# Layer 0's modulation vectors on four column groups of TensorE in half blocks, instead of VectorE ticks

## The chip, the cores and the metric

The kernel runs on one core of a Trainium2 chip. The core has TensorE (PE, matrix products; its weight loads are listed as PEld), VectorE (DVE), ScalarE (ACT), GpSimd (POOL) and a DMA queue that SyncE (SP) issues in order. The metric is the device time of one execution in microseconds (us), lower is better; a median over runs is given, and one execution is profiled.

## The reference, cut to what matters

Two layers of a trunk over 512 latent and 256 context tokens of width 1024. Each layer begins with a modulation: six vectors of 1024 for the latent tokens (from `c`) and six for the context tokens (from `c_ctx`).

```
m   = silu(c)     @ w_mod[l] + b_mod[l]      # (1024) @ (1024, 6144), split into six vectors
m_c = silu(c_ctx) @ w_mod[l] + b_mod[l]
h   = rms_norm(x, g_mix) * (1 + scale1) + shift1
x   = x + gate1 * mixer(h)                   # layer 0: SSD heads and RG-LRU blocks
h   = rms_norm(x, g_ffn) * (1 + scale2) + shift2
x   = x + gate2 * conv_ffn(h)
```

So `w_mod` of each layer, 24 MB, is read once and multiplied with two vectors only. Vectors 0 and 1 are needed before the mixer's projections, vector 2 at its output, 3 and 4 for the norm before the FFN, 5 at the FFN's output.

## The kernel before

`w_mod[l]` is cut into 24 column blocks `j` of 256 columns, four to each of the six vectors. There are three ways to compute a block.

- **On TensorE, `mod_now`** (L291): a 1 MB panel `st` is loaded, eight matmuls with the two columns `sc[:, k]` as weights and 256 columns of `w_mod` as moving data give `pmod` (2x256); VectorE copies it out (L276), two small transposes `pmodt` (L258) turn it, VectorE adds the bias (L261). Layer 0's blocks 0 to 7 go this way before the first projection, and block 21 in the output phase.
- **On VectorE, `mod_tick`** (L325): a tick loads 128 rows x 256 columns (`mst`, 128 KB, two buffers) and does two SCALAR_TENSOR_TENSORs, one for each vector, into `macc` (L83 is the helper's line). After eight ticks four matmuls with a column of ones (L352) sum over the partitions and VectorE adds the bias (L354). Layer 0's other 15 blocks (120 ticks) and all of layer 1's go this way.
- `mod_split` and `mod_vec` exist and are not used.

Work after the first norm runs in phases: the convolved projections `xbc` (from about 62 us), with the S5 tables of layer 1 and the first SSD steps woven in; the RG-LRU phase `lru_phase` (L1337), whose step for a block n projects `u` and the gate, computes four gate products (L1274, L1275), a recurrence on VectorE, ScalarE and GpSimd (L1300 to L1310) and every second n a `z` panel; the output phase `rout_phase` with the backward SSD; `project`; then FFN 0 from about 770 us. Each loop calls `mtick` with a number of ticks out of the table `MT`: one per block or step in `xbc` and `lru`, 4.5 per output block, 6 per block in `project`, 5 per step in FFN 0. The scheduler that emits the program then places each engine's instructions in an order of its own; an engine works strictly in that order, and SP too. PSUM tiles called `ps` have three buffers for `pmod`, `pmodt` and the SSD's products together.

A weight panel is loaded into `st` (two buffers), split by ScalarE (`whi`) and VectorE (`wlo`, L193), and each 128 rows of output take matmuls of 512 columns (`px`) and 256 columns (`pc`), three for each of eight k.

Of the kernel before, what the change touches and what calls it, by code (L numbers as in the profile page):

```python
# [64 lines left out]
def build(tc, I, out, dbg=None):  # L65
# [186 lines left out]
    def mod_finish(l, j, row, n, m):  # L252

        i, k0 = (j * 2) // 8, (j * 2) % 8
        r = n * m
        pt = pss("pmodt")
        for h_ in range(2):
            PE.transpose(pt[:, r * h_:r * h_ + r], row[:r, h_ * 128:(h_ + 1) * 128], ident[:r, :r])  # L258
        if m == 1:
            for h_ in range(2):  # L260
                V.tensor_scalar(MOD[l][i][:, k0 + h_, 0:n], pt[:, r * h_:r * h_ + r], P("bm", l * 48 + j * 2 + h_), None, op0=ALU.add)  # L261
        else:
            tmp = sm.tile([128, 8], F32, tag="mtmp", name="mtmp", bufs=2)
            V.tensor_copy(tmp, pt[:, :8])
            for h_ in range(2):
                stt(MOD[l][i][:, k0 + h_, :], tmp[:, 4 * h_:4 * h_ + 2], P("bm", l * 48 + j * 2 + h_), tmp[:, 4 * h_ + 2:4 * h_ + 4], ALU.add, ALU.add)
# [7 lines left out]
    def mod_row(ps, r):  # L274
        row = macc()[:, 0]
        V.tensor_copy(row[:r], ps[:r, :256])  # L276
        return row

    def mod_split(l, j, eng=None):

        w = wpanel(I["w_mod"][l], 0, 8, j * 256, 256, byk=True, eng=eng)
# [5 lines left out]
        row = mod_row(ps, 4)
        PEND.append({"l": l, "j": j, "stages": [lambda: mod_finish(l, j, row, 2, 2)]})

    def mod_now(l, j, st=None):  # L290

        if st is None:
            if (l, j) not in MODP:
                return
            st = wload(I["w_mod"][l], 0, 8, j * 256, 256)
        ps = pss("pmod")
        for k in range(8):
# [9 lines left out]

    PE_ = [j for j in range(8, 20) if (0, j) in MODP]

    def mod_pe(at):  # L310

        if at in PNS and PE_:
            k = PNS[at]
            (mod_now(0, PE_.pop(0)) if k == 1 else mod_split(0, PE_.pop(0), G if k == 2 else V))
# [41 lines left out]

    def mod_vec(l, j, st):

        acc = macc()
        for k in range(8):  # L360
            for e in range(2):
                stt(acc[:, e], st[:, k, :], sc[:, k, e:e + 1], zero.broadcast_to([128, 256]) if k == 0 else acc[:, e], ALU.mult, ALU.add)
        mod_pend(l, j, 2, acc, 1)
# [172 lines left out]
    def mod0(i):
        if START[i] == 1:
            mod_now(0, J0[i], ST0.pop(i))
        elif START[i] == 3:
            mod_vec(0, J0[i], ST0.pop(i))  # L540
        else:
            mod_split(0, J0[i], G if START[i] == 2 else V)

# [20 lines left out]
    for c in range(6):  # L564
        xturn(c)
        if c == LP0:

# [1 line left out]
            act(sc[:, :, 0], PS("c", 0, 8), AF.Silu)
            act(sc[:, :, 1], PS("cc", 0, 8), AF.Silu)  # L570
            V.tensor_copy(sc4[:, :, 0:2], sc)
            V.tensor_sub(sc4[:, :, 2:4], sc, sc4[:, :, 0:2].bitcast(F32))
# [1538 lines left out]
```

## Time and profile before

| | us |
|---|---|
| median of 3 runs (2154.59 to 2159.02) | 2155.79 |
| the profiled execution | 2153.56 |
| its span in the trace | 2151.8 |
| PE busy (94%) | 2024.4 |
| PEld busy (79%) | 1698.0 |
| DVE busy (73%) | 1573.4 |
| ACT busy (41%) | 878.2 |
| POOL busy (13%) | 278.9 |

"Busy" is the time in which at least one instruction of the engine is under way; matmuls are pipelined, so a busy PE need not be at its peak. PEclk is the clock that TensorE was granted, as a share of full speed. In the profile's page the 40 slices of PE read 8 or 9 but for a 4 in the third; those of DVE read 9 in slices 3, 5, 6 and 7. The 1.8 us between span and execution time lie outside the trace.

### The profile page before, as it was taken

How to read it: one execution, taken by the hardware profiler on the slowest of the kernel's cores; microseconds unless marked ns; L12 is line 12 of the kernel's file. 1: busy time of each engine (PE TensorE's matmuls, PEld its weight loads, DVE VectorE, ACT ScalarE, POOL GpSimd, SP SyncE). 2: the span in 40 equal slices, each digit the busy share in tenths (PEclk: the TensorE clock that was granted, in tenths of full speed). 3: DMA queues.
4: the chain of work that ended last, by engine and by line, in shares of the span. 5: the costliest groups of instructions: out<-in, count | busy, mean ns of one | idle time of the engine just before them, and what ended most of it. 6: DMA issues, size and time to landing. Idle time of an engine off the chain costs nothing.

```text
span 2151.8 us, 32734 instructions
## 1 busy us (share of the span) xinstructions
PE 2024.4 (94%) x12738; PEld 1698.0 (79%) x12738; DVE 1573.4 (73%) x2956; ACT 878.2 (41%) x1280; POOL 278.9 (13%) x240
## 2 busy tenths in 40 slices
PE   8949889888898999999999999999999899999998
PEld 4838778877677888888888888887887688888887
DVE  5897999867778888867775655665876768667484
ACT  4624577686624452212221223324444434223234
POOL 2061432334531000000000000020001100000000
PEclk9979989999899999999999999999999999999999
DMA  9425634425666414333234213455422122222221
GB/s 329 124 82 169 190 109 150 139 89 157 229 215 220 129 50 137 98 121 120 94 106 130 74 59 99 127 150 151 135 77 67 40 79 98 82 95 98 98 84 54
DMA packets 283018, 261.09 MB, mean 121 GB/s; under 512 B 23405, under 2 KB 263060, under 8 KB 282864
## 3 DMA queue, kind: packets, MB, share of 16 engines
q1 hardware_dynamic: 257504, 243.35, 35.7%
q10 hardware_dynamic: 24464, 13.75, 2.2%
q8 instruction: 100, 1.64, 0.3%
q0 software_dynamic: 896, 1.90, 0.2%
q14 instruction: 54, 0.44, 0.1%
HBM read 224.17 MB, written 34.78 MB: 120 GB/s over the span
## 4 chain that ended last, share of the span: by engine, by line
PE 62%; DVE 5%; DMA 3%; issue 2%; POOL 1%; ACT 1%; SPq 0%; POOLq 0%; DVEq 0%; ACTq 0%
PE px L215 33%; PE pc L215 10%; PE pu L215 6%; PE pseg L215 4%; DMA mst<-in_w_mod_dram 2%; DVE macc L83 1%; PE pmodt L352 1%; PE pv L222 1%; PE pv L223 1%; PE pv L224 1%; PE pob L215 1%; DMA x_d<-xo 0%; DMA Nt<-n_d 0%; DVE kx L1900 0%; PE plv L1856 0%
## 5 line engine op out<-in xcount | busy, mean ns | idle before, releaser
L80 ACT ACTIVATE whi<-st 128x1024 fp32r<-128x1024 f32 (+1 forms) x197 | 203.4, 1037 | 562.8 <-PE pc L215 367.0
L215 PE MATMUL px<-HH,whi 128*128 128x512 f32 (+2 forms) x1016 | 408.9, 404 | 19.1 <-DVE xbct L83 11.7
L215 PE MATMUL px<-HL,whi 128*128 128x512 f32 (+2 forms) x1016 | 404.6, 399 | 0.8 <-DVE HL L83 0.8
L215 PE MATMUL px<-HH,wlo 128*128 128x512 f32 (+2 forms) x1016 | 404.9, 399 | 0.0
L193 DVE TENSOR_TENSOR wlo<-st,whi 128x1024 fp32r<-128x1024 f32 (+1 forms) x197 | 238.5, 1213 | 77.6 <-ACT whi L80 75.5
L83 DVE SCALAR_TENSOR_TENSOR macc<-mst,sc,macc 128x256 f32<-128x256 f32 x434 | 218.4, 534 | 68.9 <-DMA mst<-in_w_mod_dram 68.0
L83 DVE SCALAR_TENSOR_TENSOR fa<-px,par,fa 128x441 f32<-128x441 f32 (+2 forms) x352 | 241.8, 691 | 8.2 <-ACT fa L80 2.2
L215 PEld LDWEIGHTS px<-HH,whi 128*128 128x128 f32 (+1 forms) x1016 | 192.7, 190 | 63.5 <-DVE xbct L83 12.1
L215 PEld LDWEIGHTS px<-HL,whi 128*128 128x128 f32 (+1 forms) x1016 | 192.6, 190 | 44.8 <-DVE HL L83 1.9
L215 PEld LDWEIGHTS px<-HH,wlo 128*128 128x128 f32 (+1 forms) x1016 | 192.4, 189 | 44.1
L215 PE MATMUL pc<-HH,whi 128*128 128x256 f32 x728 | 207.9, 287 | 14.1 <-DVE xbct L83 7.7
L215 PE MATMUL pc<-HL,whi 128*128 128x256 f32 x728 | 206.8, 285 | 0.0
L215 PE MATMUL pc<-HH,wlo 128*128 128x256 f32 x728 | 206.5, 284 | 0.0
L215 PEld LDWEIGHTS pc<-HH,whi 128*128 128x128 f32 x728 | 137.9, 190 | 18.5 <-issue 11.0
L80 ACT ACT_TABLE_LOAD x108 | 138.6, 1283 | 25.9 <-issue 6.2
L215 PEld LDWEIGHTS pc<-HL,whi 128*128 128x128 f32 x728 | 138.0, 190 | 1.2
L215 PEld LDWEIGHTS pc<-HH,wlo 128*128 128x128 f32 x728 | 137.7, 189 | 0.5
L215 PE MATMUL px<-fhi,wlo 128*128 128x512 f32 x304 | 120.4, 396 | 0.0
L215 PE MATMUL px<-fhi,whi 128*128 128x512 f32 x304 | 120.3, 396 | 0.0
L215 PE MATMUL px<-flo,whi 128*128 128x512 f32 x304 | 119.9, 394 | 0.0
L1813 POOL TENSOR_TENSOR kc<-kc,e 128x255 f32<-128x255 f32 x6 | 7.1, 1182 | 858.0 <-ACT kc L80 679.6
L215 PE MATMUL pu<-HH,wlo 128*128 128x512 f32 (+1 forms) x192 | 74.3, 387 | 0.0
(618 smaller groups left out, 4295.4 us busy)
## 6 DMA issues: line engine op xcount, KB each, us to landing
mst<-in_w_mod_dram SPq DMA_DIRECT2D x312, 128.0 KB, 2.1
st<-in_ffn_w_gate_dram SPq DMA_DIRECT2D x22, 1024.0 KB, 4.9
st<-in_ffn_w_up_dram SPq DMA_DIRECT2D x22, 1024.0 KB, 5.0
st<-in_ev_w_in_dram SPq DMA_DIRECT2D x18, 1024.0 KB, 6.3
st<-in_ffn_w_down_dram SPq DMA_DIRECT2D x16, 1024.0 KB, 5.0
bc<-cum_d SPq DMA_DIRECT2D x24, 512.0 KB, 6.1
sth<-in_od_w_in_dram SPq DMA_DIRECT2D x24, 512.0 KB, 4.0
st<-in_w_mod_dram SPq DMA_DIRECT2D x9, 1024.0 KB, 10.2
```

The lines of the kernel that those rows point to most:

```text
L80: return S.activation(o, i, f, bias=bias, scale=scale, **kw)
L83: return (eng or V).scalar_tensor_tensor(o, a, s, b, op0=op0, op1=op1)
L193: (eng or V).tensor_sub(lo, src, hi.bitcast(F32))
L215: PE.matmul(o, ww[:, k, :M], hh[k][part][:, sl], start=(first and q == 0 and a == 0), stop=(stop and q == last and a == 2))
L222: PE.matmul(o, hh[k][0][:, sl], whi[:, k % 4, :], start=(k == 0), stop=False)
L223: PE.matmul(o, hh[k][0][:, sl], wlo[:, k % 4, :], start=False, stop=False)
L224: PE.matmul(o, hh[k][1][:, sl], whi[:, k % 4, :], start=False, stop=(k == 7))
L352: PE.matmul(pt[:, 2 * h_ + e:2 * h_ + e + 1], acc[:, e, h_ * 128:(h_ + 1) * 128], ones[:, 0:1], start=True, stop=True)
L1813: G.tensor_mul(kc[:, 0, 0:255], kc[:, 0, 0:255], e0[:, 0:255])
```

## The change

Layer 0 leaves the ticks. Every block of layer 0 is now computed by `mod_half`, in two halves of 128 columns. The weights are 32 columns wide (`sc32`, of which two are not zero), and the eight matmuls of a half go to four column groups of TensorE (`tile_position=(0, 32q)`), two accumulating in each; the output is a 128x128 tile with four partial sums. ScalarE copies it to `mrow`, TensorE transposes it (128x128), VectorE sums the four parts (TENSOR_REDUCE) and adds the bias. Blocks 0 to 7 take their data from the same 1 MB panels as before; blocks 8 to 23 take 32 halves of 512 KB from a new buffer `mcol`, of which there is one. Two of three steps of `lru_phase` issue a half, then each output block; `xbc` issues none. Layer 1 keeps its ticks, and its pool `modp` is opened after `project` instead of at the start; in `xbc`, `lru`, `rout` and `project` there are no ticks any more, and the last four blocks of layer 1 that `out_first` named (and skipped) are dropped.

```diff
-MT = (1, 1, 4.5, 5, 1, 6, 1)
+MT = (5, 1)
-MODP = [(0, 21)]
+    HALVES = [(j, h_) for j in (8, 9, 10, 11, 16, 17, 18, 19, 12, 13, 14, 15, 20, 21, 22, 23) for h_ in range(2)]
...
+    def mod_half(l, j, h_, st):
+        if st is None:
+            st = mrp.tile([128, 8, 128], F32, tag="mcol", name="mcol", bufs=1)
+            c0 = j * 256 + h_ * 128
+            SP.dma_start(st, I["w_mod"][l, :, c0:c0 + 128].rearrange("(k p) c -> p k c", p=128))
         ps = pss("pmod")
         for k in range(8):
-            PE.matmul(ps[:2, :256], sc[:, k, :], st[:, k, :], start=(k == 0), stop=(k == 7))
-        row = mod_row(ps, 2)
+            q = k % 4 * 32
+            PE.matmul(ps[q:q + 32, :128], sc32[:, k, :], st[:, k, :], start=(k < 4), stop=(k >= 4), tile_position=(0, q))
+        row = mrp.tile([128, 128], F32, tag="mrow", name="mrow", bufs=2)
+        act(row, ps[:, :128], AF.Copy)
+        def finish():
+            pt = pss("pmodt")
+            PE.transpose(pt[:, :128], row, ident)
+            tmp = sm.tile([128, 2], F32, tag="mtmp", name="mtmp", bufs=2)
+            V.tensor_reduce(tmp, pt[:, :128].rearrange("p (q r) -> p r q", q=4)[:, 0:2, :], axis=mybir.AxisListType.X, op=ALU.add)
+            V.tensor_scalar(MOD[l][i][:, k0 + h_, :], tmp, P("bm", l * 48 + j * 2 + h_), None, op0=ALU.add)
...
-    MODSEQ = [(l, j) for l in range(2) for j in range(8 - 8 * l, 24) if (l, j) not in MODP]
+    MODSEQ = [(1, j) for j in range(24)]
...
+    def mod_at(go):
+        for q in list(PEND):
+            mod_advance(q)
+        if go and HALVES:
+            j, h_ = HALVES.pop(0)
+            mod_half(0, j, h_, None)
...
-                mtick(MT[0] if XI[0] >= SSD0 - 4 else MT[4])
+                mod_at(False)
...
-            mtick(MT[1])
+            mod_at(at % 3 < 2)
...
-        mod_now(0, 21)
...
-                mtick(MT[2])
+                mod_at(True)
```

On TensorE, at the start of the program: `pmod` is a panel's product, `pmodt` its transpose, `px` and `pc` the first projection. Before, then now:

```order
L428 MATMUL pnc<-diag,ones 128x256
L298 MATMUL pmod<-st,sc 2x256 x8
L258 MATMUL pmodt<-ident,macc 128x2 x2
L215 MATMUL px<-HH,whi 128x512
L215 MATMUL pc<-HH,whi 128x256
L215 MATMUL px<-HL,whi 128x512
```

```order
L408 MATMUL pnc<-diag,ones 128x256
L214 MATMUL px<-HH,whi 128x512 x2
L275 MATMUL pmod<-st,sc_114 32x128 x8
L284 MATMUL pmodt<-ident,mrow 128x128
L275 MATMUL pmod<-st,sc_114 32x128 x8
L284 MATMUL pmodt<-ident,mrow 128x128
L214 MATMUL px<-HL,whi 128x512
```

A panel is two groups of eight matmuls with a wide transpose each, and the projection begins one panel earlier.

On SP, where the RG-LRU phase begins: `gw` are the gate weights of a block, `st` a 1 MB weight panel, `yp_d` and `bc` belong to the SSD. Before, then now:

```order
L1126 DMA yp_d<-y 128x512
L322 DMA mst<-in_w_mod_dram 128x256
L182 DMA st<-in_ev_w_in_dram 128x8x256
L322 DMA mst<-in_w_mod_dram 128x256 x5
L1266 DMA gw<-in_lru_w_a_dram 128x2x128
L1267 DMA gw<-in_lru_w_i_dram 128x2x128
```

```order
L1066 DMA bc<-cum_d 128x8x128
L271 DMA mcol<-in_w_mod_dram 128x8x128
L1236 DMA gw<-in_lru_w_a_dram 128x2x128
L1237 DMA gw<-in_lru_w_i_dram 128x2x128
L181 DMA st<-in_ev_w_in_dram 128x8x256
L271 DMA mcol<-in_w_mod_dram 128x8x128 x2
L181 DMA st<-in_ev_w_in_dram 128x8x256
```

Small loads that waited for VectorE have gone from between the panels; larger ones that wait for TensorE stand there.

On DVE, in the recurrence of the third RG-LRU block: `gate` and `a` are its tiles. Before, then now:

```order
L1105 TENSOR_TENSOR bc<-bc,dtv 128x1024 x2
L83 SCALAR_TENSOR_TENSOR macc<-mst,sc,macc 128x256 x7
L83 SCALAR_TENSOR_TENSOR gate_3580<-a_3633,gate_3580 128x768
L83 SCALAR_TENSOR_TENSOR macc<-mst,sc,macc 128x256 x3
L83 SCALAR_TENSOR_TENSOR gate_3591<-a_3636,gate_3591 128x768
L83 SCALAR_TENSOR_TENSOR macc<-mst,sc,macc 128x256 x2
L1301 TENSOR_TENSOR gate_3602<-gate_3602,gate_3580 128x768
```

```order
L286 TENSOR_REDUCE mtmp<-pmodt 128x2 x2
L287 TENSOR_SCALAR mod_2_99<-mtmp,par_91 128x2 x2
L1217 TENSOR_TENSOR ulo<-u,uhi 128x768
L82 SCALAR_TENSOR_TENSOR gate_3464<-a_3511,gate_3464 128x768
L1239 TENSOR_TENSOR glo<-gw,ghi 128x512
L192 TENSOR_TENSOR wlo<-st,whi 128x1024
L82 SCALAR_TENSOR_TENSOR gate_3475<-a_3514,gate_3475 128x768
```

The ticks between the links of the recurrence are gone; four small instructions stand ahead of it.

## Rows read from the trace of the kernel before

**Rows 1.** Windows by phase: stretch, length, busy time of each engine, clock, DMA share, GB/s.

```profile
0.00:62.00 62.00, 54.49 (x265) 30.52 (x265) 37.29 (x136) 26.14 (x44) 11.61 (x31) 0.97 0.83 286
62.00:175.00 113.00, 80.96 (x464) 63.72 (x463) 99.54 (x288) 47.96 (x66) 42.15 (x54) 0.85 0.39 113
175.00:250.00 75.00, 71.33 (x453) 60.46 (x452) 63.75 (x99) 40.89 (x59) 20.31 (x16) 0.98 0.70 204
250.00:340.00 90.00, 78.29 (x436) 66.50 (x435) 83.25 (x117) 62.33 (x81) 32.74 (x19) 0.92 0.36 111
340.00:420.00 80.00, 70.75 (x444) 62.16 (x444) 70.61 (x87) 55.91 (x74) 28.20 (x17) 0.98 0.43 134
420.00:570.00 150.00, 131.34 (x838) 115.14 (x836) 104.03 (x103) 105.53 (x143) 67.05 (x39) 0.95 0.48 148
570.00:700.00 130.00, 117.52 (x622) 92.01 (x621) 105.76 (x229) 52.93 (x91) 33.89 (x26) 0.95 0.70 230
700.00:775.00 75.00, 74.99 (x392) 63.36 (x392) 64.43 (x178) 32.82 (x66) 0.00 (x0) 0.98 0.39 126
```

**Rows 2.** The same windows for tile macc alone: PE, PEld and DVE busy.

```profile
62.00:175.00 113.00, 0.00 (x0) 0.00 (x0) 6.84 (x16) 0.85 0.39 113
175.00:250.00 75.00, 1.00 (x8) 0.97 (x8) 6.15 (x12) 0.98 0.70 204
250.00:340.00 90.00, 2.00 (x16) 2.02 (x16) 23.18 (x36) 0.92 0.36 111
340.00:420.00 80.00, 2.01 (x16) 1.98 (x16) 24.08 (x32) 0.98 0.43 134
570.00:700.00 130.00, 5.03 (x42) 5.07 (x42) 37.90 (x75) 0.95 0.70 230
```

**Rows 3.** Chain of waits, 570 to 700 us: shares of it by line.

```profile
by line: issue 17.4%; DVE macc L83 11.2%; DMA mst<-in_w_mod_dram 10.6%; DMA x_d<-xo 7.5%; PE px L215 5.4%; DMA st<-in_ev_w_out_dram 4.2%; POOL hs L1078 3.5%; DMA xo<-xT_d 3.4%; POOL xw L1066 3.2%; DVE wlo L83 2.8%; PE pc L215 2.7%; POOL zy 
```

**Rows 4.** Timeline of PE, 37 to 53 us: start, length, line, tiles, count.

```profile
38.95 3.62 PE L298 MATMUL pmod<-st,sc 128*2 128x256 f32 x16
42.50 0.28 PE L258 MATMUL pmodt<-ident,macc 2*128 2x2 f32 x2
```

**Rows 5.** Timeline of PE, 1475 to 1477 us: a layer 1 product on column groups.

```profile
1475.51 0.71 PE L1834 MATMUL psc<-vth,ktc 128*128 128x128 f32 x4
1476.15 0.46 PE L1856 MATMUL plv<-q,ks 128*32 128x32 f32 x32
1476.54 0.39 PE L215 MATMUL pc<-HL,whi 128*128 128x256 f32 x1
```

**Rows 6.** Groups by form, ACT and DVE: small copies out of PSUM, bias.

```profile
L80 ACT ACTIVATE S<-psc 128x128 f32<-128x128 f32 x12 | 3.3, 278 | 8.9 <-PE psc L1834 8.9
L354 DVE TENSOR_SCALAR mod<-pmodt,par 128x2 f32<-128x2 f32 x46 | 8.1, 211 | 1.1 <-PE pmodt L352 1.1
```

**Rows 7.** Timeline of SP: the stores of RG-LRU blocks 1, 3 and 5.

```profile
338.29 0.32 SPq L1311 DMA_DIRECT2D r_d<-gate  x1
419.11 0.32 SPq L1311 DMA_DIRECT2D r_d<-gate  x1
491.86 0.34 SPq L1311 DMA_DIRECT2D r_d<-gate  x1
```

**Rows 8.** DMA issues: count, KB each, median us to landing.

```profile
bc<-cum_d SPq DMA_DIRECT2D x24, 512.0 KB, 6.1
sth<-in_od_w_in_dram SPq DMA_DIRECT2D x24, 512.0 KB, 4.0
```

**Rows 9.** Chain of waits, in FFN 1: 24 matmuls of 512 columns.

```profile
1906.54 5.60 PE pu L215 x24
```

**Rows 10.** Timelines of DVE and POOL, 360 to 368 us.

```profile
362.66 5.25 DVE L83 SCALAR_TENSOR_TENSOR macc<-mst,sc,macc 128x256 f32<-128x256 f32 x5
362.28 4.16 POOL L1300 TENSOR_TENSOR gate<-gate,u 128x768 f32<-128x768 f32 x2 [0.36 <-ACT gate L80]
```

More of the change, by code (lines that the diff above doesn't have):

```diff
@@ L38 @@
 ME0 = 10
-PNS = {}
 UB = 2
@@ L75, in build @@
     mp_ctx = ExitStack()
-    mp = mp_ctx.enter_context(tc.tile_pool(name="modp", bufs=2, reuse_waits="tile"))
+    mp = None
+    mr_ctx = ExitStack()
+    mrp = mr_ctx.enter_context(tc.tile_pool(name="modr", bufs=2, reuse_waits="tile"))
     dr = es.enter_context(tc.tile_pool(name="dram", bufs=1, space=DRAM))
@@ L244, in mod_need @@
     def mod_need(l, i):
+        while l == 0 and any(j // 4 == i for j, _ in HALVES):
+            mod_at(True)
         while any((a, b // 4) == (l, i) for a, b in MODSEQ[TICK[0] // NQ:]):
@@ L250, in mod_need @@
                 mod_advance(q)
[L252 to L266, printed above, removed]
     def macc():
@@ L272, in macc, with mod_cols @@
         return mp.tile([128, 2 if LIM[0] < len(MODSEQ) else 1, 256], F32, tag="macc", name="macc", bufs=2)
[L274 to L281, printed above, removed]
+    def mod_cols(l, j, st=None):
+        for h_ in range(2):
+            src = None if st is None else st[:, :, h_ * 128:(h_ + 1) * 128]
+            mod_half(l, j, h_, src)
@@ L287, in mod_split @@
[L287 to L297, printed above, removed]
-            PE.matmul(ps[:2, :256], sc[:, k, :], st[:, k, :], start=(k == 0), stop=(k == 7))
-        row = mod_row(ps, 2)
-        PEND.append({"l": l, "j": j, "stages": [lambda: mod_finish(l, j, row, 2, 1)]})
@@ L303, in build @@
+        PEND.append({"l": l, "j": j, "stages": [lambda: None, finish]})
+    MODSEQ = [(1, j) for j in range(24)]
     NQ = 8
@@ L306, in build @@
     MACC = []
[L308 to L314, printed above, removed]
+    def mod_at(go):
[4 more added lines that the diff above has]
+            mod_half(0, j, h_, None)
     def mod_load():
@@ L355, in mod_pend @@
         PEND.append({"l": l, "j": j, "stages": [lambda: None] * lag + [finish]})
[L357 to L363, printed above, removed]
     def gscale(l, which, i):
@@ L527, in build @@
     xin, ST0 = [], {}
-    sc = cp.tile([128, 8, 2], F32, name="sc")
-    sc4 = cp.tile([128, 8, 4], F32R, name="sc4")
+    sc32 = cp.tile([128, 8, 32], F32, name="sc32")
+    G.memset(sc32, 0.0)
     par0 = fetch_par(0, ldp, S)
     def st0(i):
-        if START[i] in (1, 3):
-            ST0[i] = wload(I["w_mod"][0], 0, 8, J0[i] * 256, 256, tag="stm")
+        ST0[i] = wload(I["w_mod"][0], 0, 8, J0[i] * 256, 256, tag="stm")
     def mod0(i):
[L537 to L542, printed above, removed]
+        mod_cols(0, J0[i], ST0.pop(i))
     def xturn(c):
@@ L568, in build @@
             turn_par(*par0)
[L569 to L572, printed above, removed]
+            act(sc32[:, :, 0], PS("c", 0, 8), AF.Silu)
+            act(sc32[:, :, 1], PS("cc", 0, 8), AF.Silu)
         if c in M0C and m0 < n1:
@@ L1523, in build @@
     rest = norm.early()
-    project(panel, h, range(8), X, T, 0, 2, stats, full, early=rest, mid=lambda q: wsts["mid"](q), tick=lambda: mtick(MT[5]))
+    project(panel, h, range(8), X, T, 0, 2, stats, full, early=rest, mid=lambda q: wsts["mid"](q), tick=lambda: mod_at(True))
     def done0():
+        nonlocal mp
         sp_ctx.close()
         es0.close()
+        mr_ctx.close()
+        mp = mp_ctx.enter_context(tc.tile_pool(name="modp", bufs=2, reuse_waits="tile"))
+        mod_load()
     for k in range(8):
@@ L1602, in build @@
     FP = []
-    ffn(0, X, T, norm, rest, wfirst, done0, h, nxt0, chain(l1_consts(), (mtick(MT[3]) for j in range(38 + 4 * PSG))))
+    ffn(0, X, T, norm, rest, wfirst, done0, h, nxt0, chain(l1_consts(), (mtick(MT[0]) for j in range(38 + 4 * PSG))))
     norm, rest, pools = FP
@@ L1989, in out_first @@
                 yield
-        for j in range(16, 20):
-            mod_now(1, j)
-            yield
     with tc.tile_pool(name="s5p", bufs=1, side="right", reuse_waits="tile") as ap:
```

16 lines of the change are left out of this document (6 added, 10 removed).

## The prediction

> **What bounds the kernel now.** I read the windows by phase first [rows 1]. From 700 us on TensorE is full (74.99 of 75 us), so little can be won there. Before that it is not: its idle time is 7.5 us of 0 to 62, 32.0 of 62 to 175, 3.7 of 175 to 250, 11.7 and 9.3 of the next two, 18.7 of 420 to 570 and 12.5 of 570 to 700, together 95 us. DVE is busy for 88% and 85% of 62 to 250, 93% and 88% of 250 to 420, 69% of 420 to 570 and 81% of 570 to 700. So up to 420 us and in the output phase DVE is near its limit; between 420 and 570 neither engine is, and the pace comes from the chain of the RG-LRU recurrence and the SSD over several engines. Next, how much of DVE is the modulation: the same windows for `macc` alone [rows 2] give 6.8, 6.2, 23.2, 24.1 and 37.9 us. There are no ticks from 420 to 570. In 340 to 420 one costs 24.08 / 32 = 0.75 us against 6.15 / 12 = 0.51 before 250. Last, the chain in the output phase [rows 3]: `macc` has 11.2% of 130 us and the wait for its 128 KB loads 10.6%, 28 us together. That is the strongest sign that the ticks cost time.
>
> **The price of a half.** Eight FP32 matmuls are 16 instructions, two passes each. `pmod` before takes 3.62 us for 16 of 256 columns [rows 4], so 0.87 ns a column: 16 of 128 columns would take 1.78 us one after another. The only product on column groups in the trace is `plv` [rows 5]: 32 instructions of 32 columns, which at 0.87 ns would need 0.89 us in series, start and are followed by the next product within 0.39 us. With four at a time they need 0.22 us, and the other 0.17 us is the change over. `psc` ahead of it needs 4 x 128 x 0.87 = 0.45 us and `plv` starts 0.64 us after it, so the way in may cost up to 0.19 us more. A half is then 1.78 / 4 + 0.2 = 0.65 us, between 0.6 and 0.85; in series it would be 2.0.
> The Trainium skill, TensorEngine Tiling (Array Packing), Key Properties, says that a change of tiling mode drains TensorE; the trace agrees by those 0.17 to 0.36 us. The same page, PSUM Bottleneck, says that tiling does not speed up taking results out of PSUM; here that side does grow, as the next sentence works out.
> Behind the matmuls come a ScalarE copy of 128x128 (0.28 us [rows 6]), a 128x128 transpose (taken as 0.28 us, that of the small one [rows 4]; its 2 x 128 columns at 0.87 ns are 0.22), a TENSOR_REDUCE to 128x2, of which the trace has no small one (0.21 us like the bias, between 0.15 and 0.4), and the bias (0.21 [rows 6]). So a half costs PE 0.93, ACT 0.28, DVE 0.42 us, each with its waits.
>
> **The change by phase.** Against the profiled execution's 2153.56 us; the median of the runs is 2.2 us above it.
> - 0 to 62: eight panels go from 3.62 + 0.28 = 3.90 us of PE to 2 x 0.93 = 1.86. The panel at 38.95 and two behind it lie between matmuls of the first projection, so 3 x 2.04 = 6.1 us leave a full PE; the earlier ones wait for loads. But the norm's work on DVE stays, and it feeds this projection. I take -4 (-8 to 0).
> - 62 to 250: 13.0 us of DVE go and nothing comes. DVE is near its limit, yet part of these ticks sits in waits. I take -5, 40% (-13 to 0).
> - 250 to 570: 47.3 us of ticks go. How much of that was on the path shows in the stores of RG-LRU blocks 1, 3 and 5 [rows 7]: the pair with 32 instructions of ticks took 80.8 us, the pair without 72.8. That is 8 us for a pair, 16 for the two pairs' worth of ticks in 250 to 420. In their place come 24 halves: 22.3 us of PE, less about 4 us of `macc`'s products [rows 2], 18.3 net, where PE idles 12 to 13%; I let 40% of it count, +8. The one buffer adds waits: load n+1 can be issued only when half n has been multiplied. Two halves of three follow each other across a block's four gate products, 12 matmuls of 512 and 12 of 256 columns, at 0.233 us [rows 9] and half of it 4.2 us of PE. A 512 KB load with the same rows lands in 4.0 us, one in this phase in 6.1 [rows 8]. With 0.5 us for the issue the wait is 0.3 to 2.4 us at about 12 places, 4 to 29 us; PE has pauses of its own inside the gate products, so I take 0.5 each, +6. ACT's 24 x 0.28 = 6.7 us and DVE's 10 us lie beside other work: +2. Sum 0 (-25 to +25).
> - 570 to 700: 37.9 us of DVE and the waits for `mst` go; 28 us of the chain [rows 3]. What can be gained is limited by PE's idle 12.5 us and by the SSD's chain, which has shares of its own in POOL and DMA. PE gets 8 x 0.93 = 7.4 us, and loses block 21 (3.9) and about 4 of `macc`'s 5.0 us [rows 2], so it stays even. I take -9 (-18 to +3).
> - From 700: PE is full, DVE's ticks there cost it nothing, and only `macc`'s products of three blocks or so leave it: -2. Layer 1's ticks in FFN 0 keep their number per step, and their pool starts later than needed by nothing that waits for it.
> Sum: -4 - 5 + 0 - 9 - 2 = -20, so 2133.6; I say 2133.
>
> The SP queue: a `mcol` load that waits for TensorE holds up what stands behind it, a 1 MB panel and the gate weights. Before, the `mst` loads waited there for DVE in the same way, in more places; I cost the exchange at nothing beyond the waits above.
>
> One mechanism helps more than I have counted. Where a tick meets a GpSimd instruction, both are stretched: five ticks' instructions took 5.25 us beside a `gate` product on POOL of 4.16 us for two [rows 10], against 0.51 us each in 175 to 250 [rows 2]. The Trainium skill, SBUF — State Buffer, Terms, says that DVE and GpSimd hold a pair of ports exclusively for a whole instruction; the trace agrees. By it GpSimd is held up too, and freeing it shortens the recurrence: that would put the pair's gain above the 8 us, on the side of the first rival.
>
> **Rivals.**
> 1. Much faster: DVE is the limit wherever it is over 80% busy, and what it is relieved of counts in full. 13 + 47.3 + 37.9 us less DVE's new 32 x 0.42 = 13.4 gives -85; the cap is PE's idle time in these phases, 69 us up to 420 and in the output phase [rows 1], of which 62 to 175 can return no more than its 6.8 us of ticks: 44, and with 4 at the start and 2 behind 700 about -50: 2104. For it: DVE's 93% in 250 to 340 and the chain in rows 3. Against it: the pair without ticks gains only 8 us [rows 7].
> 2. Slower: the one `mcol` buffer. If loads take the 6.1 us of this phase and PE runs straight through the gate products, it waits 2.4 us at 12 places, 29 us, with SSD loads and panels behind it on SP; the rest of the sum (-20, less the 6 counted) leaves +3, and late panels another 8 to 10: 2165. It decides from a wait of 1.7 us at each place on. For it: one buffer, and SP in order. Against it: the 4.0 us of the equal load, and PE's 12% pauses.
> 3. The four groups don't overlap: 2.0 instead of 0.65 us a half, 48 x 1.35 = 65 us more PE, of which half shows: 2165. Rows 5 speak against it.
> 4. Nothing: in every phase the chain of recurrence, SSD and loads sets the pace, and ticks and halves both lie in its pauses. Then only the start and the wide products remain: 2150. For it: 69% DVE, 88% PE and still no faster in 420 to 570.
>
> **How the numbers follow.** The forecast has 0.50, rival 1 0.17, rival 2 0.15, rival 3 0.03, rival 4 0.15. What can be told apart here is 0.2% or 4.3 us, so "same" is 2151.5 to 2160.1. The forecast's own range is 2118 to 2150, all faster. Rival 1 is faster; rival 4 is half faster, half same, rivals 2 and 3 are slower with a few in a hundred the same. Faster 0.50 + 0.17 + 0.06 = 0.73, same 0.10, slower 0.17. The range reaches to rival 1 below and half way to rival 2 above: 2102 to 2157.
>
> **What would show it.** Right: `pmod` groups of 16 instructions in 0.45 to 0.65 us with four starting together; the stores of RG-LRU blocks 1 and 3 about 75 to 80 us apart; the output phase 10 us shorter with no `macc` in its chain; FFN 0 with the same length. Wrong: `pmod` waiting for DMA `mcol` for more than 15 us in total, SP waiting for `pmod` with panels late behind it, `pmod` instructions 0.11 us apart (no overlap), or a gain above 30 us in 250 to 570, which would say that DVE alone had set the pace there.

## The result, and the profile after

The changed kernel takes 2172.55 us in the median of 5 runs (2167.44 to 2172.79), the kernel before 2154.59 (2149.43 to 2159.02) in 5 runs beside it: a ratio of 1.0075, 95% interval 1.0054 to 1.0096. It is slower by 0.75%, 16 us by this ratio (the two medians lie 18 us apart), where 20 us less were forecast; the time lies above the range of 2102 to 2157. The profiled execution took 2168.25 us with a span of 2166.4.

First the windows by phase of the kernel after, which answer to [rows 1] (stretch, length, busy time of PE, PEld, DVE, ACT and POOL, granted clock, DMA share, GB/s):

```profile
0.00:62.00 62.00, 48.11 (x441) 34.71 (x442) 41.07 (x158) 32.78 (x64) 13.52 (x35) 0.92 0.93 308
62.00:175.00 113.00, 84.82 (x479) 68.17 (x478) 98.89 (x270) 50.17 (x70) 41.69 (x50) 0.85 0.35 102
175.00:250.00 75.00, 71.35 (x450) 60.54 (x449) 65.40 (x92) 42.52 (x58) 33.23 (x20) 1.00 0.72 207
250.00:340.00 90.00, 80.58 (x566) 69.08 (x567) 50.87 (x72) 61.30 (x88) 21.50 (x12) 0.96 0.43 128
340.00:420.00 80.00, 75.45 (x540) 64.02 (x539) 52.17 (x70) 54.14 (x79) 22.58 (x13) 1.00 0.47 139
420.00:570.00 150.00, 129.75 (x877) 108.43 (x875) 91.74 (x112) 100.47 (x143) 53.19 (x32) 0.91 0.47 144
570.00:700.00 130.00, 111.69 (x640) 83.47 (x638) 79.16 (x149) 56.79 (x95) 48.85 (x38) 0.89 0.72 227
700.00:775.00 75.00, 71.40 (x408) 61.39 (x406) 54.67 (x146) 33.02 (x66) 2.56 (x2) 1.00 0.37 121
```

DVE has lost its ticks: 83.25 and 70.61 us in 250 to 420 have become 50.87 and 52.17, and `macc` [rows 2] is absent up to 700 us. TensorE is busier from 62 to 420 us and less busy before and behind that. POOL, where parts of each SSD step run, has fallen from 32.74 to 21.50 in 250 to 340 and risen from 33.89 to 48.85 in 570 to 700: work of the SSD has moved to the right.

That is plainest in the stores. These rows give, for one kind of store on SP, the count, its shortest, middle and longest issue, and the times of the first and the last. `yp_d` is written by each of the 12 forward SSD steps, `r_d` by each of the 8 RG-LRU blocks, `x_d<-xo` (`x1_d` in the code) by the output phase. Of the kernel before:

```profile
L1126 SPq DMA_DIRECT2D yp_d<-y x12: 319/332/1092, 234.4 to 573.7; - x12
L1311 SPq DMA_DIRECT2D r_d<-gate x8: 319/335/339, 305.1 to 567.3; - x8
L1492 SPq DMA_DIRECT2D x_d<-xo x16: 319/346/891, 598.2 to 682.4; - x16
```

Of the kernel after:

```profile
L1096 SPq DMA_DIRECT2D yp_d<-y x12: 319/320/530, 220.0 to 597.5; - x12
L1281 SPq DMA_DIRECT2D r_d<-gate x8: 332/338/339, 288.7 to 551.8; - x8
L1459 SPq DMA_DIRECT2D x_d<-xo x16: 319/380/1338, 621.9 to 701.2; - x16
```

The RG-LRU ends 15.5 us sooner, the SSD 23.8 us later. Before, both end within 6.4 us of each other, 11 of the 12 SSD stores ahead of the last `r_d`; after, 7 are, and five steps follow alone. The output phase needs both: its first store comes 24.5 us behind the last `yp_d` before and 24.4 after. So the gain of the RG-LRU is not used, and the SSD's end sets the phase.

What stands in the 46 us between the ends shows in windows of 25 us, before and then after:

```profile
550.00:575.00 25.00, 21.18 (x140) 19.36 (x140) 14.16 (x15) 14.18 (x21) 10.03 (x8) 0.84 0.69 220
575.00:600.00 25.00, 22.51 (x93) 14.31 (x92) 21.84 (x42) 13.23 (x18) 11.13 (x8) 0.89 0.67 242
```

```profile
550.00:575.00 25.00, 17.79 (x69) 11.37 (x68) 18.90 (x20) 7.66 (x12) 16.00 (x13) 0.80 0.70 214
575.00:600.00 25.00, 14.21 (x43) 9.36 (x44) 17.96 (x22) 11.55 (x12) 16.72 (x11) 0.52 0.63 203
```

and in the chain of waits of the kernel after (start, length, engine, tile, line):

```profile
560.49 0.76 PE pcbm L1068 x2
561.25 1.71 PE pin L1055 x2
562.96 1.71 PE pst L1043 x2
564.66 2.01 PE pyi L1094 x16
...
566.75 0.69 DVE y L1095
567.44 1.15 DVE bc L1075
...
570.63 1.76 POOL hs L1048
572.39 0.21 issue
572.60 1.09 POOL bc L1077
573.68 0.93 POOL xw L1036
574.62 0.04 issue
574.65 1.26 POOL y L1089
575.91 1.00 POOL y L1084
576.91 1.98 POOL hs L1048
```

This is one SSD step after the other over PE, DVE and POOL, with no projection left to fill TensorE until 599 us; its granted clock is 0.52 from 575 to 600 us.

A half itself costs TensorE what was worked out. TensorE at 44.78 us, which answers to [rows 4], and the same half earlier:

```profile
20.45 1.08 PE L275 MATMUL pmod<-st,sc 128*32 128x128 f32 x16
...
44.78 0.64 PE L275 MATMUL pmod<-st,sc 128*32 128x128 f32 x16
45.36 0.33 PE L284 MATMUL pmodt<-ident,mrow 128*128 128x128 f32 x1
45.45 0.36 PE L214 MATMUL pc<-HH,whi 128*128 128x256 f32 x1
```

A half keeps TensorE for 0.58 us from its start to the start of the next product, as it does nearly everywhere that the clock is at its full level, and the transpose here for 0.09. The rows by tile give the rest: the copy, the sum and the bias (ns: shortest, middle, longest).

```profile
L79 ACT ACTIVATE mrow<-pmod x48: 250/273/280, 16.1 to 698.0; 128x128 f32<-128x128 f32 x48
L286 DVE TENSOR_REDUCE mtmp<-pmodt x47: 135/159/168, 20.6 to 714.5; 128x2 f32<-128x8 f32 x47
L287 DVE TENSOR_SCALAR mod<-mtmp,par x47: 219/224/1902, 20.8 to 715.4; 128x2 f32<-128x2 f32 x47
```

The loads land in 4.2 us, between the two of [rows 8]:

```profile
mcol<-in_w_mod_dram SPq DMA_DIRECT2D x32, 512.0 KB, 4.2
```

Two of the waits of TensorE from 240 to 600 us (who, for what, us in total, times, longest); the longest in that list is 6.4 us in all:

```profile
PE pmod L275 <- DMA mcol<-in_w_mod_dram: 4.9, 4, 3.6
PE pst L1043 <- DVE mtmp L286: 3.3, 1, 3.3
```

and the largest of SP's queue from 240 to 700:

```profile
SPq L271 <- PE pmod L275: 70.6, 17, 12.1
```

TensorE hardly waits for the loads; SP waits much ahead of them, and the RG-LRU's panels and gate weights stand behind. The stores of its blocks 1, 3 and 5, which answer to [rows 7], are

```profile
318.16 0.34 SPq L1281 DMA_DIRECT2D r_d<-gate  x1
...
396.41 0.34 SPq L1281 DMA_DIRECT2D r_d<-gate  x1
...
479.39 0.33 SPq L1281 DMA_DIRECT2D r_d<-gate  x1
```

78.3 and 83.0 us apart (80.8 and 72.8 before): the pair that had ticks is 2.5 us shorter, the pair that had none 10.2 us longer. The second line on TensorE's waits is the odd one: `pst` is a product of the SSD, `mtmp` the sum of a half. They share no data, only the three PSUM tiles called `ps`.

### The profile page after: what moved, and what is told of

Its sections match the earlier page's. It is cut to its first block, busy times and chain, and to the rows that moved or that the text cites. A ratio compares the mean times of both kernels' runs of the same rounds, so it can differ in the third digit from the quotient of the medians.

```text
span 2166.4 us, 33490 instructions
## 1 busy us (share of the span) xinstructions
PE 2029.8 (94%) x13272; PEld 1706.4 (79%) x13272; DVE 1472.0 (68%) x2753; ACT 890.8 (41%) x1329; POOL 282.5 (13%) x241
## 4 chain that ended last, share of the span: by engine, by line
PE 69%; DVE 14%; DMA 5%; ACT 4%; POOL 4%; issue 3%; SPq 1%; ACTq 0%; POOLq 0%; DVEq 0%
PE px L214 36%; PE pc L214 12%; PE pu L214 6%; PE pseg L214 4%; ACT L79 1%; DMA mst<-in_w_mod_dram 1%; DVE wlo L192 1%; ACT gate L79 1%; PE pz L222 1%; PE pz L223 1%; PE pz L221 1%; DVE xbct L82 1%; DVE gate L1271 1%; DVE u L82 1%; PE pmod L275 1%
## 5 line engine op out<-in xcount | busy, mean ns | idle before, releaser
L79 ACT ACT_TABLE_LOAD x109 | 139.8, 1283 | 28.2 <-DVE xbct L82 12.6
L214 PEld LDWEIGHTS pc<-HH,whi 128*128 128x128 f32 x728 | 138.2, 190 | 10.2 <-ACT ge L79 5.6
L82 DVE SCALAR_TENSOR_TENSOR macc<-mst,sc,macc 128x256 f32<-128x256 f32 x224 | 102.1, 479 | 45.3 <-DMA mst<-in_w_mod_dram 44.3
## 6 DMA issues: line engine op xcount, KB each, us to landing
mcol<-in_w_mod_dram SPq DMA_DIRECT2D x32, 512.0 KB, 4.2
bc<-cum_d SPq DMA_DIRECT2D x24, 512.0 KB, 6.0
sth<-in_od_w_in_dram SPq DMA_DIRECT2D x24, 512.0 KB, 4.3
```

The lines of the kernel that those rows point to most:

```text
L79: return S.activation(o, i, f, bias=bias, scale=scale, **kw)
L82: return (eng or V).scalar_tensor_tensor(o, a, s, b, op0=op0, op1=op1)
L214: PE.matmul(o, ww[:, k, :M], hh[k][part][:, sl], start=(first and q == 0 and a == 0), stop=(stop and q == last and a == 2))
```

## The experiments

Theory "order": the halves take turns with the SSD's products for the `ps` tiles, so SSD steps written behind the halves can't be emitted ahead of them. (At `SSDR = 0.15` a piece of the SSD is written about every 6.7 steps of the RG-LRU phase, and what is left behind its last block.) Rivals: the one buffer and SP's queue ("queue"), TensorE's added work ("work"). All ratios are to the kernel before, on the same chip, with 95% intervals. "End" is the later of the last `r_d` and the last `yp_d` store, "phase" the time from the last `xbct` to it, "SSD" the number of `yp_d` stores ahead of the last `r_d`. All times in us, of one profiled execution.

| kernel | ratio | last xbct | last r_d | last yp_d | SSD | phase | x_d stores |
|---|---|---|---|---|---|---|---|
| before | 1 | 240.1 | 567.3 | 573.7 | 11 | 334 | 598 to 682 |
| after | 1.0075 (1.0054 to 1.0096) | 230.7 | 551.8 | 597.5 | 7 | 367 | 622 to 701 |
| e1 px | 1.0004 (0.9989 to 1.0019) | 231.7 | 582.6 | 513.3 | 12 | 351 | 610 to 688 |
| e2 SSDR | 1.0046 (1.0034 to 1.0058) | 233.0 | 582.6 | 594.0 | 11 | 361 | 618 to 705 |
| e3 one load | 1.0034 (1.0021 to 1.0046) | 230.0 | 555.0 | 600.7 | 7 | 371 | 625 to 697 |
| e4 before, SSDR | 1.0058 (1.0035 to 1.0081) | 240.5 | 592.3 | 571.0 | 12 | 352 | 623 to 695 |
| e5 start only | 1.0009 (0.9999 to 1.0020) | 237.3 | 568.3 | 574.5 | 11 | 337 | 599 to 684 |
| e6 px, one load | 0.9965 (0.9950 to 0.9980) | 232.8 | 580.9 | 533.0 | 12 | 348 | 610 to 685 |
| e7 px 12/12/8 | 0.9998 (0.9988 to 1.0008) | 234.7 | 585.1 | 537.2 | 12 | 350 | 608 to 688 |
| e8 px 12/20/0 | 0.9959 (0.9944 to 0.9974) | 238.6 | 579.7 | 588.4 | 10 | 350 | 616 to 685 |
| e9 ps 12/20/0 | 1.0054 (1.0039 to 1.0068) | 241.8 | 562.7 | 606.9 | 7 | 365 | 631 to 697 |
| e10 px, 64 KB | 1.0014 (1.0001 to 1.0026) | 233.7 | 583.0 | 514.2 | 12 | 349 | 612 to 687 |
| e11 px 24/0/8 | 1.0009 (0.9998 to 1.0021) | 263.8 | 572.8 | 583.3 | 10 | 320 | 613 to 693 |
| e12 px 24/8/0 | 1.0066 (1.0054 to 1.0079) | 259.2 | 603.0 | 554.6 | 12 | 344 | 632 to 701 |
| e13 e8, one load | 1.0031 (1.0016 to 1.0045) | 241.2 | 576.6 | 591.1 | 9 | 350 | 625 to 696 |
| e14 px 12/16/0, 4 | 0.9990 (0.9975 to 1.0004) | 238.0 | 588.5 | 567.0 | 12 | 351 | 621 to 687 |
| e15 none | 0.9873 (0.9848 to 0.9897) | 230.0 | 543.2 | 527.1 | 12 | 313 | 572 to 656 |
| e16 pc | 1.0048 (1.0031 to 1.0066) | 233.9 | 569.0 | 590.4 | 9 | 357 | 621 to 699 |
| e17 px 12/first 8/8, 4 | 0.9935 (0.9907 to 0.9963) | 242.1 | 570.8 | 573.3 | 11 | 331 | 598 to 682 |
| e18 px 12/every second/8, 4 | 0.9979 (0.9966 to 0.9993) | 233.6 | 570.1 | 551.5 | 12 | 336 | 600 to 681 |

Figures such as 12/20/0 are the halves in `xbc`, in the RG-LRU phase and in the output phase (0/24/8 in the changed kernel); a fourth stands for `project`.

**Is it the PSUM tiles?** e1 gives the loaded halves other tiles and changes nothing else:

```diff
     def mod_half(l, j, h_, st):
+        pps = psx if st is None else pss
...
-        ps = pss("pmod")
+        ps = pps("pmod")
...
-            pt = pss("pmodt")
+            pt = pps("pmodt")
```

> The changed kernel, with pmod and pmodt of the 32 loaded halves in the PSUM tiles px instead of ps. Theory 'order': the halves take turns with the SSD's products for the three ps tiles in the order in which the program was written, so the SSD steps written behind the halves can't be emitted ahead of them; without that, at least 10 of the 12 yp_d stores (7 after the change, 11 before) lie ahead of the last r_d store, the hole of TensorE at 550 to 600 us (14 of 25 us busy) closes, the first x1_d store comes at 605 us or earlier (621.9) and the time is 2150 to 2160. Rival 'queue' (one mcol buffer, SP held up by its loads): loads and waits stay, 2168 to 2173. Rival 'work' (24 halves of TensorE work and changes of tiling): same work, 2168 or more.

The loss against the kernel before is gone (1.0004), with the loads, the buffer and the work as they were, and all 12 SSD steps end before the RG-LRU:

```profile
L1097 SPq DMA_DIRECT2D yp_d<-y x12: 319/530/1892, 221.0 to 513.3; - x12
L1282 SPq DMA_DIRECT2D r_d<-gate x8: 319/336/339, 290.6 to 582.6; - x8
```

Against "queue" and "work" as the cause of the 0.75% that decides. But two of the numbers were missed: the first `x_d` store comes at 609.8, not 605, and TensorE's hole hasn't closed (12.64 of 25 us busy from 575 to 600). The last `r_d` comes 31 us later than in the changed kernel, so the phase falls from 367 to 351 us only, still 17 longer than before. The backward SSD, too, has moved ahead into this phase: its first load, `zy<-yp_d`, is issued at 461.8 us (542.7 before, 512.0 in e15 below). Whether that is what delays the RG-LRU no run shows by itself. e16 puts the halves into the third family of tiles (`pps = psc ...`):

> The changed kernel with pmod and pmodt of the loaded halves in the PSUM tiles pc (two buffers, shared with the 256-column products). Theory 'order': what counts is how the SSD stands among the blocks; here five of its steps stand behind the seventh block's gates, so it falls between the changed kernel and e1, 2160 to 2170 (ratio 1.002 to 1.006). If sharing with the projections' tiles costs in itself, every product with two column widths waits for the halves: 2172 or more.

It falls in between, and so does the order: 9 SSD stores ahead of the last `r_d`, 1.0048.

**Is it enough to write the SSD earlier?** `SSDR = 0.28` instead of 0.15, in the changed kernel (e2) and in the kernel before (e4):

> The changed kernel with SSDR 0.28 instead of 0.15: the SSD steps are written about every 3.6 steps of the RG-LRU phase instead of every 6.7, all 12 within it. Theory 'order': this too takes the SSD out from behind the halves; the RG-LRU phase itself gets longer by 5 to 10 us, the rows after it come sooner, 2148 to 2160. Rival 'queue': SSD loads and mcol loads meet more often, 2170 or more. Rival 'work': 2168 to 2173.

> The kernel before with SSDR 0.28: a control for e2. Theory 'order': before, the scheduler moves the SSD steps ahead by itself, as no ticks run after 420 us, so writing them earlier changes little, 2148 to 2162. If it gains as much as e2 does over the changed kernel (12 us or more), the place of the SSD steps is a gain apart from this change.

No: e2's phase is still 361 us, its time 6 us above the forecast of "order". The kernel before loses 0.58% by the same edit: its RG-LRU ends 25 us later. So writing the SSD earlier can cost the RG-LRU more than it gains; e15, next, shows an early SSD beside an RG-LRU that is not late.

**What the RG-LRU phase costs without any modulation.** e15 issues no half there (`mod_at(False)`) and leaves 20 out:

> The changed kernel with no halves in the RG-LRU phase: eight halves in the output phase and four in project, the other 20 not computed (their modulation is zero, not the reference's). This is the stage without modulation, xbc as in the changed kernel. If the halves are what made the phase long, it takes 315 to 325 us from the last xbct (367 in the changed kernel, 334 before), 10 or more yp_d stores lie before the last r_d store, and the time is 2120 to 2135. If it is still 345 or more, the phase is long for another reason (the start, xbc, the missing mst loads), and the time stays above 2150.

```profile
L79 ACT ACTIVATE xbct<-xbct x12: 843/845/856, 64.1 to 230.0; 128x768 f32<-128x768 f32 x12
L1099 SPq DMA_DIRECT2D yp_d<-y x12: 319/320/798, 219.2 to 527.1; - x12
L1284 SPq DMA_DIRECT2D r_d<-gate x8: 319/320/338, 289.5 to 543.2; - x8
L1462 SPq DMA_DIRECT2D x_d<-xo x16: 320/383/1152, 572.0 to 656.0; - x16
```

The phase takes 313 us. From the last `xbct` to the last `r_d` it is 313.2 here, 321.1 in the changed kernel and 327.2 before: the ticks cost the RG-LRU 14.0 us, the 24 halves 7.9. The last `yp_d` is 70.4 us earlier than in the changed kernel. But the 7.9 is no price of the halves alone, as five SSD steps fewer stand among the blocks of the changed kernel than of e15. Taken as a whole, to the later end, the phase is 53.6 us shorter without the halves, 2.2 us for each. e1 gives back 15.9 of these. The other 37.7 are there in e1 although in e1 and in e15 all 12 SSD steps stand ahead of the last `r_d`. TensorE in that phase, e1 and then e15 (columns as in [rows 1]):

```profile
231.70:582.60 350.90, 316.66 (x2159) 266.89 (x2158) 252.13 (x296) 232.58 (x327) 148.79 (x86) 0.94 0.50 151
230.00:543.20 313.20, 285.50 (x1738) 247.44 (x1738) 228.57 (x239) 227.34 (x303) 133.32 (x79) 0.96 0.41 126
```

It is busy for 31.2 us more in e1; `pmod` and `pmodt` have 24.8 (18.3 and 6.4), two thirds of the 37.7. But 8 or 12 halves cost the phase nearly as much as 24 (e12 and e7 below), so it is no price by the half.

**The loads.** e3 keeps one of the 32 loads; gates, SSD steps and halves follow each other on TensorE as in the changed kernel up to the output phase, though some single products between them have moved; e6 and e13 do the same to e1 and e8; e10 keeps SP's waits in e1 but loads an eighth:

```diff
-        if st is None:
+        if st is None and MC:
+            st = MC[0]
+        elif st is None:
...
+            MC.append(st)
```

> The changed kernel with one mcol load instead of 32: all halves multiply the first one's weights, so what it leaves out is 31 loads of 512 KB and every wait on SP and TensorE for them (layer 0's modulation of blocks 8 to 23 is then not the reference's). TensorE's order stays that of the changed kernel. Theory 'order': the SSD stays late (first x1_d store 612 to 622 us), and the time is within 5 us of the changed kernel, 2166 to 2173. Rival 'queue': the loss goes, 2150 or less. Rival 'work': 2168 to 2173.

> e1 with one mcol load instead of 32 (all halves multiply the first one's weights: the modulation of blocks 8 to 23 is not the reference's). Theory 'parts add': in e1 the order is mended and what the loads cost is left, about the 9 us that e3 gained: 2147 to 2152. Rival 'one cause': e1 and e3 took away the same loss, so no more than 3 us below e1, 2155 to 2159. Rival 'work': what is left in e1 is TensorE's 24 halves in the RG-LRU phase; its length from the last xbct to the last r_d store (351 us in e1, 327 before) stays within 5 us of e1's.

> e8 with one mcol load instead of 32 (all loaded halves use the first one's weights: the modulation of blocks 8 to 23 is not the reference's). If a half costs the RG-LRU phase by its load (SP held up, late panels, waits of TensorE), the phase of e8 (350 us from the last xbct to the later of the last r_d and last yp_d store) falls by 10 us or more and the ratio to 0.991 or less. If by its work on TensorE and ACT and by the order, the phase stays above 343 and the ratio at 0.993 to 0.996.

> e1 with loads of 64 KB in place of 512 KB (only the first 128 rows, which all eight matmuls of a half use, so that the modulation of blocks 8 to 23 is not the reference's): SP still waits for TensorE ahead of each load, the traffic is an eighth. If the traffic and the landing cost the 0.4% between e1 and e6, it runs like e6, ratio 0.995 to 0.998, 2146 to 2152. If SP's waits cost it, it stays like e1, 0.999 to 1.002, 2154 to 2160.

e3 keeps the late SSD and gains 0.4%, 9 us, more than the 5 that "order" allowed and far less than "queue" wanted; its phase is no shorter, and its output phase takes 72 us from first to last store instead of 79. e6 repeats the 0.4% on e1. e10 gains nothing with an eighth of the traffic; but its FFN 0, where no half runs, takes 541.2 us in the trace against 535.0 in e1 (layer 1's ticks start later there), so it doesn't tell the traffic from SP's waits. But e13 is 0.7% slower than e8: without the loads the order came out otherwise (9 SSD stores instead of 10, the output phase 8 us later). The removal of a load moves instructions as well, so the loads' own price stays open; it is not the main loss.

**The start alone.** e5 is the kernel before with `mod_cols` for blocks 0 to 7 only; from the middle of the `xbc` phase on each engine's order is that of before:

```diff
-            mod_now(0, J0[i], ST0.pop(i))
+            mod_cols(0, J0[i], ST0.pop(i))
```

> The kernel before with only the start changed: blocks 0 to 7 on four column groups in half blocks; blocks 8 to 23 of layer 0 keep VectorE's ticks, and TensorE's order after the start is that of the kernel before. Theory 'parts add': the start is worth the 9 to 10 us by which the first and last xbct come earlier in e1 to e3, the following phases keep their lengths, 2146 to 2150 (ratio 0.995 to 0.998). Rival 'cover': the 9 us are lost again in the RG-LRU phase or given back in FFN 0, 2154 to 2157.

The first `xbct` comes 7.6 us sooner (59.5), the last 2.8, the last `r_d` store 1.0 later: nothing is left, as "cover" had it. In the changed kernel, where the ticks in `xbc` go too, the last `xbct` stays 9.4 us sooner.

**Where the halves stand.** e7, e8 and e9 move 12 to `xbc`; e8 and e9 differ only in the tiles:

```diff
-                mod_at(False)
+                mod_at(True)
...
-            mod_at(at % 3 < 2)
+            mod_at(at % 9 < 5)
```

> e1 with 12 halves in the xbc phase (one per block), 12 in the RG-LRU phase (every third step) and 8 in the output phase. If TensorE's work or the loads set the RG-LRU phase, that phase gets 6 to 12 us shorter; xbc, where TensorE idles 28 of 113 us, gets at most 5 us longer: 2148 to 2156. If VectorE's near-full xbc phase pays for each half (copy, sum, bias and waits), xbc gets 10 us or more longer and nothing is won: 2157 to 2163.

> e1 with 12 halves in xbc, 20 in the RG-LRU phase (five of nine steps) and none in the output phase, whose loads of 512 KB stand on SP among the xo, r_d and SSD loads. If the loads in the output phase cost the 7 us by which that phase was shorter in e3 (first to last x1_d store 71.9 against 79.3 us), it takes 72 us or less here (78.1 in e1): 2148 to 2155. If not, its length stays at 78, and 2155 to 2162.

> e8's places for the halves (12 in xbc, 20 in the RG-LRU phase, none in the output phase) with pmod and pmodt in the ps tiles, as in the changed kernel: the order is not mended. If order and output phase are two causes that add, it keeps the order's loss: 8 or fewer yp_d stores before the last r_d store, a hole of TensorE behind it, and a time between the changed kernel and e8, 2156 to 2165 (ratio 1.001 to 1.004). If taking the halves out of the output phase was all of e8's gain, and the order none of it: 2144 to 2150.

e7 gains nothing over e1: with half the halves the phase stays at 350. e8 is faster than before, with an output phase of 69 us. e9, with the same places but `ps`, is 0.95% slower than e8, about 20 us (by the ratio of each to the kernel before, as they ran on two chips):

```profile
L1096 SPq DMA_DIRECT2D yp_d<-y x12: 319/326/1602, 234.4 to 606.9; - x12
L1281 SPq DMA_DIRECT2D r_d<-gate x8: 333/338/339, 304.3 to 562.7; - x8
```

7 stores again, a gap of 44 us, and a phase of 365 us against 350. This is the cleanest pair for the tiles: the same halves in the same steps, once in each family.

> e1 with 24 halves in xbc (two per block), none in the RG-LRU phase and 8 in the output phase. From the last xbct to the later of the last r_d and the last yp_d store the kernel before took 334 us, with ticks, e1, e6, e7 and e8 348 to 351 with 12 to 24 halves. If the halves' work and loads make that phase long, it falls to 335 or less here, as neither ticks nor halves are in it; xbc grows by 6 to 14 us; 2148 to 2160. If its length comes from how SSD and RG-LRU are interleaved by now, it stays at 345 or more, and with the longer xbc 2160 to 2170.

> e1 with 24 halves in xbc, 8 in the RG-LRU phase (every fourth step) and none in the output phase. If halves cost less in xbc than in the RG-LRU phase (12 of them lengthened xbc by 3 to 7 us in e7 and e8), it beats e8 by a few us: 2140 to 2146. If xbc is filled by the second dozen (VectorE is busy for 88% of it), each costs its full 0.9 us there, and it is e8's equal or slower: 2146 to 2156.

> e8 with 16 halves in the RG-LRU phase (four of nine steps) and the last four in project. Four halves fewer at 1.2 to 1.5 us each shorten the RG-LRU phase by 5 to 6 us, and project gets at most 4 us longer: 2142 to 2148, equal to e8 or 0.1 to 0.2% faster. If the SSD is drawn ahead again as in e1 and e12 (all 12 yp_d stores well before the last r_d store), the phase doesn't get shorter: 2148 to 2158.

In e11 the phase is 320 us without halves, but `xbc` ends 32 us later than in e1: 1.3 us a half, more than the 0.7 that TensorE is taken for. e12 shows that their number isn't what makes the phase long: eight halves take it to 344. There, as in e1, e7 and e14, all 12 SSD steps end early and the RG-LRU late; in e15 they end early as well, 16 us ahead of the last `r_d`, and the RG-LRU isn't late (543 us, 567 before), so an early SSD by itself isn't the reason.

> e1 with 12 halves in xbc, 8 in the first eight steps of the RG-LRU phase, 8 in the output phase and 4 in project. If halves hurt only where the SSD stands behind them, the phase from the last xbct takes 320 to 330 us (313 without halves in e15, 350 in e1 and e8), and with 4 to 7 us more in xbc the time is 2136 to 2146, below before and e8. If eight halves cost it as much as 24 did (e12: 344 us with 8), it is 2155 or more.

> As e17, with the 8 halves in every second of the first 16 steps of the RG-LRU phase. If they cost the phase only 1 us or so each, it takes 320 to 330 us and the time is 2136 to 2146; if the spreading over twice the steps lets the SSD fall behind or be drawn ahead (fewer than 9 or all 12 yp_d stores before the last r_d store), 340 us or more, and 2150 or more.

```diff
-            mod_at(at % 3 < 2)
+            mod_at(at < 8)
```

e17 has the lowest ratio of the kernels that compute all of it, 0.9935, 2143.57 us in the median of 7 runs (2126.05 to 2152.94); its interval overlaps that of e8. Its profiled execution is the slowest of these; the two ends meet again:

```profile
L1097 SPq DMA_DIRECT2D yp_d<-y x12: 319/326/655, 230.9 to 573.3; - x12
L1282 SPq DMA_DIRECT2D r_d<-gate x8: 319/320/339, 309.9 to 570.8; - x8
```

The phase takes 331 us, but in this trace the output phase ends where it did before (681.9 against 682.4 us): `xbc` ends 2.0 us later, and 9.2 of the 9.7 us that are won up to layer 1 lie in `project` and FFN 0. With the same eight halves spread over 16 steps (e18) the SSD runs ahead, the phase takes 336 us instead, and the gain is 0.2%.

## Why the prediction was wrong, step by step

| step | predicted | profile |
|---|---|---|
| start, to the first `xbct` | -4 | -9.6 |
| `xbc`, to the last `xbct` | -5 | +0.2 |
| RG-LRU, to the last `r_d` | 0 (-16 ticks, +16 halves) | -6.1 (-14.0 ticks, +7.9 halves) |
| SSD's end behind it | no term | +39.3 (6.4 to 45.7) |
| output phase, to the last `x_d` | -9 | -5.0 |
| `project`, to the first `fa` of FFN 0 | -2 with FFN 0 | -6.6 |
| FFN 0 | | -7.3 |
| layer 1 | 0 | +9.7 |
| sum | -20 | +14.6 |

- The price of a half held: 0.58 instead of 0.65 us of products, 0.09 instead of 0.28 for the transpose, 0.27 on ACT, 0.38 instead of 0.42 on DVE. Rival 3 (no overlap) is out.
- The step "How much of that was on the path shows in the stores of RG-LRU blocks" came near in its sum for the ticks: 16 us of ticks predicted, 14.0 measured by e15, 13.7 of it up to the store of block 3, where the ticks stood. The reading of the pairs held less well, and here luck helped: without any ticks and halves they take 75.8 and 78.1 us (80.8 and 72.8 before), so the first gains 5.0, not 8, and the second, which never had ticks, is not a measure of a pair without them. It held, too, that TensorE's waits for `mcol` are short (4.9 us against 6 predicted).
- The step that failed is the sum for 250 to 570, "Sum 0". It took the RG-LRU's stores as the length of the phase and charged the halves (+8, +6 and +2) to the RG-LRU alone. The phase ends with the later of two chains, and the halves went into the SSD's tiles: the SSD's end, 39.3 us in the table, has no term. To the later end the halves cost 53.6 us (e15) where 16 were charged. Of these 15.9 us (0.7%) are shown to come from the shared tiles, by e1; e9 against e8 has 15.3 us of phase and 0.95%. The other 37.7 us are left when the order is freed, because the RG-LRU then ends later, and the phase is hardly shorter without the loads (e6: 348 us). So without the tiles the forecast would have failed too: e1 comes to 1.0004, not to 20 us less. The 24.8 us that TensorE spends on the halves are near the 22.3 of the prediction, of which, less 4 for `macc`'s products, it let 40% count; what the rest is stays open.
- That the tiles are shared was to be seen: the text ahead of the prediction says that `ps` has three buffers for `pmod`, `pmodt` and the SSD together, and [rows 2] has no tick from 420 to 570, where before six of the 12 `yp_d` stores fall. The prediction's own sign of being right, blocks 1 and 3 at 75 to 80 us, came true (78.3): it sees the RG-LRU alone.
- Rival 2 had the side right and the mechanism wrong. SP did wait for `pmod`, 70.6 us in all, but without the loads (e3) the RG-LRU ends no sooner, at 555.0 us against 551.8. What e3 gains, 9 us, shows in the output phase, not at 12 places among the gates.
- Rivals 1 and 4 are both out. With no modulation in the phase (e15, 0.9873) it gets 20.4 us shorter than before: less than half of the 47.3 us that DVE is relieved of, and not nothing.
- The output phase gained 5.0 of the 9 us forecast. Its chain by line, which answers to [rows 3], has no `macc` any more, but a wait for `mcol` in place of that for `mst` (570 to 700 us, so its first 27 us are the SSD's tail):

```profile
by line: issue 22.7%; PE px L214 16.1%; PE pc L214 8.4%; DMA x_d<-xo 5.6%; POOL hs L1048 4.3%; POOL xw L1036 3.9%; DMA mcol<-in_w_mod_dram 3.7%; PE pin L1055 3.6%; POOL y L1089 3.5%; DMA rlo<-r_d 3.4%; PE pst L1043 3.3%; POOL zy L1131 3.0%;
```

- From 700 us on, "-2" was too little: `project` and FFN 0 give 13.9 us. From 700 to 1340 us `macc`'s products take 12.6 us of TensorE instead of 17.3 (104 instructions for 144), and DVE runs 208 tick instructions instead of 278; what makes the rest of the gain no run shows. The 9.7 us lost in layer 1 are mostly none of the change's: e5, which has the instructions of before there, loses 7.3 against the same profiled execution while its ratio is 1.0009, and all other runs take 825.6 to 833.0 us there against 823.7 in the trace of before.
- Start and `xbc` came out right as a sum (-9.4 for -9) by luck: both terms are 5 us off, in opposite directions. And e5 shows that they don't stand by themselves: with the ticks left in `xbc`, the start's gain is gone before the last `r_d`.

## What to carry to other kernels

Before work is put into a phase, list which rotating buffers it shares, and which later-written work would have to overtake it: PSUM tiles borrowed for 24 products of 0.6 us cost about 16 us by where they put another chain's instructions. Where two chains share a phase, measure both ends and sum against the later one; a gain on the other is not used, and freeing one can delay the other. A removed load or product also moves the rest, so an experiment on cost should show that the order stayed the same.

## What the runs showed of the hardware

- Eight FP32 matmuls of 128 columns on four column groups, changes of tiling included, hold TensorE for 0.58 us, against 3.62 us for the 256-column product of before [rows 4]; so a panel went from 3.62 to twice 0.58 us for its products. The Trainium skill, TensorEngine Tiling (Array Packing), PSUM Bottleneck, says that tiling speeds up TensorE but not the way out of PSUM; the trace agrees, with 0.27 us for each half's copy, twice for a panel, against 0.40 us for the one copy before. Here one thing more counted: the tile itself was what the neighbours lacked.
- The clock showed in the same instructions: a half at 20.45 us, at a granted clock of 0.50, is listed with 1.08 us, one at 44.78 us, at 1.00, with 0.64. From 575 to 600 us, in the SSD's lone tail, the granted clock was 0.52, near the lower of its two levels (1.2 of 2.4 GHz), after TensorE had been busy for 17.79 of 25 us; it was 0.89 at that place before.
- Not settled: what makes 37.7 us of the phase in e1, why 8, 12 and 24 halves cost it nearly the same (344, 350 and 351 us), why a half costs 1.3 us in `xbc` (e11) when TensorE, ACT and DVE are taken for 0.7, 0.3 and 0.4 us, and what the loads cost by themselves.
